# HGRN2 scores of distance 1 and 2 from channel products and a matrix of ones, in a streaming encoder step

## The chip, the cores and the metric

The kernel runs on one core of a Trainium2 chip. The metric is the time of one execution on the device, in microseconds (us). Three runs of the kernel before took 1739.62, 1742.65 and 1743.55 us; their median, 1742.65 us, is the time before.

## What is computed

The reference is one layer of a streaming encoder: an input projection of 2048 prompt frames and 8 x 16 sample frames, stick-breaking attention in 8 heads, an HGRN2 recurrence in 4 heads of 128 channels, an output projection and a LayerNorm. The change touches the HGRN2 part alone:

```
b = jnp.cumsum(gc, axis=2)                                  # g = log f
diff = b[:, :, :, None, :] - b[:, :, None, :, :]
decay = jnp.where(causal, jnp.exp(jnp.minimum(diff, 0.0)), 0.0)
scores = jnp.einsum('bhtd,bhsd,bhtsd->bhts', qc, kc, decay)
o = (jnp.einsum('bhts,bhsv->bhtv', scores, ic)
     + jnp.einsum('bhtd,bhdv->bhtv', qc * jnp.exp(b), S))
```

A score of the pair (s, t) is a sum over 128 channels of q[t] k[s] times the product of the forget gates f after s up to t.

## The kernel before, in words

The program has three stages: the input projection with the HGRN2 work woven into it (to about 1000 us), the stick-breaking attention, and the output projection. Only the first is touched.

**Projection.** The frames are taken in two halves. Each half has three tiles of tokens: 384, 384 and 384 in the first (the last 128 of these are the sample frames), 384, 384 and 256 in the second. The list `order` holds sections of 128 output columns (FH, QH, GH of a head, KA, QA, GA of attention) or of 256 (IH, VA). Each tile of a section takes 24 fp32r matmuls, since weight and input are split in a rounded part and a rest: 128x384 at L313 to L315, or 128x256 at L323 to L325 for IH and VA. After each 9, 9 and 6 of the first kind, or each 12 of the second kind, the loop calls `weave`. After the first tile of a section, `split_w` splits the weights of the next one: ScalarE copies (L109, `wh`), GpSimd takes the difference (L117, `wl`): two pairs of 128x512 for a section of 128 columns, four for one of 256. Sections KA and QA also split their output in this way (`e`).

**Chains.** When the GH section of a head is done, three generators `hgrn` are appended to `chains`, one per tile. `weave` takes the next step (up to the next `yield`) of the first chain, then puts that chain behind the second one. So two chains, here called A and B, go step by step in turn, and the third, C, begins when they end and goes alone, one step per `weave`. There are 4 heads x 2 halves = 8 pairs and 8 lone chains, 24 in all. All instructions are queued in the order in which Python issues them (`manual_schedule`), and each engine takes its own in that order.

**Levels.** A chunk of 128 tokens is worked level by level with distances m = 1, 2, 4, ..., 64. In each level, `scores` multiplies kS and q of a chunk in full fp32 (a 128x128 matmul, L430, two instructions each), then VectorE scales half of q and half of kS by the gate products of that level (L455, L456), keeps those scores that belong to the level by a mask (`copy_predicated`, L447) and forms the next gate products (L459). The diagonal is handled apart: the product dp = q kS (L423) is split in dh (ScalarE, fp32r) and dl = dp - dh (GpSimd, L466), and after the last level two matmuls with a matrix of ones sum dh and dl over the channels (L469, L470), masked into the scores at L471. The tile `ps` of these matmuls has two buffers for all chains together.

Of the kernel before, what the change touches and what calls it, by code (L numbers as in the profile page):

```python
# [9 lines left out]
F32 = mybir.dt.float32  # L10
F32R = mybir.dt.float32r
# [37 lines left out]
def constants():  # L49
    i = np.arange(P)  # L50
    s, t = i[:, None], i[None, :]
    x = s ^ t
    lev = np.stack([(s < t) & (x >= m) & (x < 2 * m) for m in LEVELS[:NL]] + [s == t], 1)
# [12 lines left out]
def stream_step_kernel(ctx: ExitStack, tc: tile.TileContext, x_prompt, x_sample, cache_k, cache_v, state_s,  # L66
# [19 lines left out]
    lev = cst.tile([P, NL + 1, P], U8, name="lev")  # L86
    hmask = cst.tile([P, H], F32, name="hmask")

    qT_d = scr.tile([4, 2, P, T], F32, name="qT_d")
# [44 lines left out]
    def bc(ap, n):  # L134
        return ap.unsqueeze(2).to_broadcast([ap.shape[0], ap.shape[1], n])
# [29 lines left out]
    def at(step, fn):  # L165
        todo.setdefault(max(step, -LZ - 9), []).append(fn)
# [31 lines left out]
    with ExitStack() as ph:  # L198
# [206 lines left out]
        def hgrn(half, h, hg, t0, nch):  # L405
# [13 lines left out]
            dp = hw.tile([P, TW], F32, name="dp", tag="kN")[:, :n]  # L419
            dh = hw.tile([P, TW], F32R, name="dh", tag="dh")[:, :n]  # L420
            dl = hw.tile([P, TW], F32R, name="dl", tag="dl")[:, :n]
            pool.memset(sc[:, :nch], 0.0)
            dve.tensor_tensor(dp, q, kS, ALU.mult)  # L423
            dve.tensor_tensor(q, q, f, ALU.mult)
            yield

            def scores(k):
                ps = psc.tile([P, 4, P], F32, name="ps", tag="ps")
# [1 line left out]
                    mm(ps[:, c], ch(kS, c), ch(q, c), start=True, stop=True)  # L430
                return ps[:, :k]

            tot = f
            tot16 = None
            for li, m in enumerate(LEVELS):
                k = nch if m < TS else npr
                if m < BLK:
                    ps = scores(k)
                else:
                    ps = psc.tile([P, 4, P], F32, name="ps", tag="ps")  # L440
                    for s0_ in range(0, P, 2 * m):
                        for c in range(k):
                            mm(ps[s0_:s0_ + m, c, :m], kS[:, c * P + s0_:c * P + s0_ + m],
                               q[:, c * P + s0_ + m:c * P + s0_ + 2 * m], start=True, stop=True)
                def keep_scores():
                    if m < BLK:
                        dve.copy_predicated(sc[:, :k], lev[:, li:li + 1].to_broadcast([P, k, P]), ps)  # L447
# [4 lines left out]
                q4 = q[:, :nn].rearrange("p (b two m) -> p b two m", two=2, m=m)  # L452
                k4 = kS[:, :nn].rearrange("p (b two m) -> p b two m", two=2, m=m)
                t3 = tot[:, :nn // m].rearrange("p (b two) -> p b two", two=2)
                dve.tensor_tensor(q4[:, :, 1], q4[:, :, 1], bc(t3[:, :, 0], m), ALU.mult)  # L455
                dve.tensor_tensor(k4[:, :, 0], k4[:, :, 0], bc(t3[:, :, 1], m), ALU.mult)  # L456
                keep_scores()
                nt = hw.tile([P, TW // 2 // m], F32, name=f"tot{m}", tag=f"tot{m}")[:, :nn // (2 * m)]
                dve.tensor_tensor(nt, t3[:, :, 0], t3[:, :, 1], ALU.mult)  # L459
                tot = nt  # L460
                if m == 8:
                    tot16 = nt
# [78 lines left out]


        def small():
            levf = xr.tile([P, NB, P], F32, name="levf", tag="x")[:, :NL + 1]
# [757 lines left out]
```

## Time and profile before

| | us |
|---|---|
| median of three runs | 1742.65 |
| lowest, highest | 1739.62, 1743.55 |
| the profiled execution | 1747.05 |
| its span, first to last instruction | 1745.2 |

The profiled execution is 4.40 us above the median, and 1.85 us of its time lie outside its span. Its page lists the busy time of the engines: PE is TensorE's matmuls, PEld its weight loads, DVE VectorE, ACT ScalarE, POOL GpSimd, SP the queue that issues the DMAs. Matmuls are pipelined, and the time of one is that from its start to its last result, so the rate is read from the distance of their starts. The mean granted TensorE clock of the execution is 0.989 of full speed.

### The profile page before, as it was taken

The page shows a single profiled execution, that of the slowest core. Times are in us where ns is not written, and L with a number is a line of the kernel's source. Part 1 is how long each engine was busy: PE and PEld are TensorE (multiplying, and loading weights), DVE is VectorE, ACT ScalarE, POOL GpSimd, SP SyncE. Part 2 cuts the span into 40 slices and gives each one's busy share as a digit, 9 for nine tenths or more (in the row PEclk, how much of TensorE's full clock was granted, in tenths as well). Part 3 has the DMA queues.
Part 4 walks back from the last instruction along what each step waited for, and adds up shares of the span by engine and source line. Part 5 has one row for each costly group of instructions (what it writes and reads, how often), then busy time and mean ns, then how long its engine had stood idle before and what let it go on. Part 6 is the DMA issues. An engine that isn't in the chain of part 4 may idle for free.

```text
span 1745.2 us, 33561 instructions
## 1 busy us (share of the span) xinstructions
PE 1672.4 (96%) x12901; PEld 1519.8 (87%) x12901; DVE 971.0 (56%) x1762; ACT 710.9 (41%) x1641; POOL 776.6 (44%) x870
## 2 busy tenths in 40 slices
PE   8999999999989999999999978999999999999998
PEld 8999999999989999999999966877887777778886
DVE  4264444255634263641647337787887686665554
ACT  3231221221323132221223246777877897775110
POOL 1242313232341142221323346777777776665664
PEclk9999999999999999999999989999999999999999
DMA  4233132122345133231212388899795754431443
GB/s 156 62 108 105 61 98 81 41 72 67 94 129 166 37 110 87 67 111 43 73 51 90 111 208 168 195 206 237 166 222 123 216 160 113 100 89 60 133 146 115
DMA packets 298790, 204.12 MB, mean 117 GB/s; under 512 B 113532, under 2 KB 275848, under 8 KB 298632
## 3 DMA queue, kind: packets, MB, share of 16 engines
q1 hardware_dynamic: 298632, 201.98, 43.5%
q8 instruction: 103, 1.69, 0.4%
q14 instruction: 55, 0.45, 0.1%
HBM read 146.36 MB, written 56.10 MB: 116 GB/s over the span
## 4 chain that ended last, share of the span: by engine, by line
PE 81%; DVE 5%; ACT 4%; DMA 4%; issue 2%; POOL 2%; SPq 1%; POOLq 0%; DVEq 0%; ACTq 0%
PE pj L313 10%; PE pj L315 10%; PE pj L314 10%; PE po L795 6%; PE z L742 5%; PE wt L777 5%; PE ps L430 4%; PE pj L323 4%; PE pj L325 4%; PE pj L324 4%; PE py L1132 3%; PE py L1134 3%; PE py L1133 3%; PE pk L877 2%; DVE kS L456 2%
## 5 line engine op out<-in xcount | busy, mean ns | idle before, releaser
L313 PE MATMUL pj<-xh,wh 128*128 128x384 f32 (+1 forms) x1152 | 395.7, 343 | 0.0
L764 POOL TENSOR_TENSOR s<-s,pr 128x512 f32<-128x512 f32 (+3 forms) x320 | 324.1, 1019 | 120.0 <-DVE pr L711 97.9
L315 PE MATMUL pj<-xh,wl 128*128 128x384 f32 (+1 forms) x1152 | 376.2, 327 | 0.0
L314 PE MATMUL pj<-xl,wh 128*128 128x384 f32 (+1 forms) x1152 | 375.7, 326 | 0.0
L117 POOL TENSOR_TENSOR wl<-wr,wh 128x512 fp32r<-128x512 f32 x126 | 164.2, 1327 | 387.9 <-ACT wh L109 387.9
L711 DVE TENSOR_TENSOR_SCAN pr<-keep,pr,one 128x513 f32<-128x513 f32 x192 | 238.6, 1270 | 46.7 <-ACT keep L750 35.0
L313 PEld LDWEIGHTS pj<-xh,wh 128*128 128x128 f32 x1152 | 217.4, 189 | 3.0 <-issue 1.0
L314 PEld LDWEIGHTS pj<-xl,wh 128*128 128x128 f32 x1152 | 217.5, 189 | 0.7 <-issue 0.7
L315 PEld LDWEIGHTS pj<-xh,wl 128*128 128x128 f32 x1152 | 216.7, 188 | 0.0
L742 PE MATMUL z<-kst,qr 128*128 128x512 f32 (+3 forms) x640 | 187.6, 404 | 17.9 <-ACT keep L750 6.3
L109 ACT COPY wh<-wt 128x512 f32<-128x512 f32 (+3 forms) x320 | 165.9, 550 | 78.4 <-PE wt L777 76.7
L747 ACT ACTIVATE s<-z 128x512 f32<-128x512 f32 (+3 forms) x320 | 184.6, 577 | 16.3 <-PE z L744 9.7
L777 PE MATMUL wt<-ident,s 128*128 128x128 f32 x1088 | 165.0, 279 | 2.1 <-POOL s L764 1.9
L323 PE MATMUL pj<-wh,xh 128*128 128x256 f32 x544 | 161.2, 296 | 0.0
L324 PE MATMUL pj<-wl,xh 128*128 128x256 f32 x544 | 153.0, 281 | 0.8 <-POOL wl L117 0.8
L777 PEld LDWEIGHTS wt<-ident,s 128*128 128x128 f32 x1088 | 123.2, 142 | 34.9 <-issue 16.4
L325 PE MATMUL pj<-wh,xl 128*128 128x256 f32 x544 | 152.8, 281 | 0.0
L117 POOL TENSOR_TENSOR e<-ev,e 128x384 fp32r<-128x384 f32 (+1 forms) x48 | 45.3, 943 | 221.1 <-ACT e L109 152.4
L795 PEld LDWEIGHTS po<-wh,vst 128*64 128x64 f32 x2176 | 119.1, 138 | 26.4 <-issue 16.2
L742 PEld LDWEIGHTS z<-kst,qr 128*128 128x128 f32 x640 | 106.0, 197 | 39.7 <-ACT keep L750 19.9
L795 PE MATMUL po<-wh,vst 128*64 128x128 f32 x2176 | 138.5, 279 | 0.0
L750 ACT ACTIVATE keep<-z 128x512 f32<-128x512 f32 (+2 forms) x230 | 134.6, 585 | 0.0
(164 smaller groups left out, 2907.0 us busy)
## 6 DMA issues: line engine op xcount, KB each, us to landing
wr<-in_w_in SPq DMA_DIRECT2D x64, 512.0 KB
qr<-qT_d SPq DMA_DIRECT2D x64, 256.0 KB
kr<-in_cache_k SPq DMA_DIRECT2D x16, 1024.0 KB
vr<-in_cache_v SPq DMA_DIRECT2D x32, 512.0 KB
kst<-kT_d SPq DMA_DIRECT2D x24, 512.0 KB
mt<-mx_d SPq DMA_DIRECT2D x136, 64.0 KB
x<-in_x_prompt SPq DMA_DIRECT2D x16, 512.0 KB
out<-xr SPq DMA_DIRECT2D x16, 512.0 KB
```

What stands on the lines that cost most here:

```text
L117: eng_lo.tensor_tensor(lo, src, f32(hi), ALU.subtract)
L313: mm(o, wh[:, k], xh[:, k, :n], start=k == 0, stop=False)
L314: mm(o, wh[:, k], xl[:, k, :n], start=False, stop=False)
L315: mm(o, wl[:, k], xh[:, k, :n], start=False, stop=k == KT - 1)
L323: mm(o, xh[:, k, ts], wh[:, k], start=k == 0, stop=False)
L324: mm(o, xh[:, k, ts], wl[:, k], start=False, stop=False)
L325: mm(o, xl[:, k, ts], wh[:, k], start=False, stop=k == KT - 1)
L711: dve.tensor_tensor_scan(pr[:, CW - wd:CW + 1][:, ::-1], kr, by, carry, ALU.mult, ALU.bypass)
L742: mm(z[:, :wd], q[:, a, r, q0:q0 + P], k[:, a, k0:k0 + wd], start=r == 0, stop=r == 1 and not top)
L764: pool.tensor_tensor(s[:, :wd], s[:, :wd], pr[:, CW - wd + 1:CW + 1], ALU.mult)
L777: nc.tensor.transpose(pt_[:, x:x + P], U[(u, a)][0][:, x:x + P], ident)
L795: mm(o[r], v[:, lo // P % 8 + x, r], th[a][:, x * P:(x + 1) * P], start=top and x == 0, stop=bot and x == n - 1, skip_group_check=True)
```

## The change

The scores of levels 1 and 2 are no longer taken from full matmuls. For level 1, the elementwise product of the odd tokens' q and the even tokens' kS (half the columns) is split in dh and dl and summed over channels by two matmuls with the matrix of ones. For level 2, there are four pairs per block of four tokens, so the product has as many columns as the tile. A column sum stands in all 128 rows of the result, and masks pick the row of s for each t: one `copy_predicated` for level 1, two per chunk for level 2. The diagonal's sums move from the last step to the first ones, and the same three tiles dp, dh, dl now serve all three sums in turn (`split` is the copy on ScalarE and the difference on GpSimd of the kernel before). Levels from 4 up are as before. The number of steps of a chain stays the same.

```diff
-            dve.tensor_tensor(dp, q, kS, ALU.mult)
+            def parts(w, out, a, b):
+                dve.tensor_tensor(out, a, b, ALU.mult)
+                split(act, pool, dh[:, :w], dl[:, :w], dp[:, :w])
+
+            def sums(w):
+                ps = psc.tile([P, 4, P], F32, name="ps", tag="ps").rearrange("p c t -> p (c t)")[:, :w]
+                mm(ps, ones, dh[:, :w], start=True, stop=False)
+                mm(ps, ones, dl[:, :w], start=False, stop=True)
+                return ps
+
+            def pick(i, out, cols, data):
+                dve.copy_predicated(out, lev[:, i, cols].unsqueeze(1).to_broadcast([P, nch, 64]), data)
...
+            parts(n, dp[:, :n], q, kS)
             dve.tensor_tensor(q, q, f, ALU.mult)
             yield
+            ps = sums(n)
+            dve.copy_predicated(sc[:, :nch], lev[:, 0:1].to_broadcast([P, nch, P]), ps.rearrange("p (c t) -> p c t", t=P))
+            parts(n // 2, dp[:, :n // 2], pair(q)[:, :, 1], pair(kS)[:, :, 0])
+            scale(n, 1, pair(f))
+            tot = total(1, n, pair(f))
+            yield
+            ps = sums(n // 2)
+            pick(1, sc[:, :nch, 1::2], slice(1, P, 2), ps.rearrange("p (c t) -> p c t", t=64))
+            q4, k4 = (z.rearrange("p (b two m) -> p b two m", two=2, m=2) for z in (q, kS))
+            sh = [P, n // 4, 2, 2]
+            parts(n, dp[:, :n].rearrange("p (b t s) -> p b t s", t=2, s=2),
+                  q4[:, :, 1].unsqueeze(3).to_broadcast(sh), k4[:, :, 0].unsqueeze(2).to_broadcast(sh))
+            scale(n, 2, pair(tot))
+            tot = total(2, n, pair(tot))
+            yield
+            ps = sums(n).rearrange("p (b t s) -> p b t s", t=2, s=2)
+            s4 = sc[:, :nch].rearrange("p c (b two t) -> p (c b) two t", two=2, t=2)
+            for a in range(2):
+                m4 = lev[:, 2 + a].rearrange("p (b two t) -> p b two t", two=2, t=2)[:, :, 1]
+                for c in range(nch):
+                    bs = slice(c * 32, (c + 1) * 32)
+                    dve.copy_predicated(s4[:, bs, 1], m4, ps[:, bs, :, a])
...
             for li, m in enumerate(LEVELS):
+                if m < 4:
+                    continue
...
-                if m == 2:
-                    copy(act, dh, dp)
-                if m == 4:
-                    pool.tensor_tensor(dl, dp, f32(dh), ALU.subtract)
                 yield
-            ps = psc.tile([P, 4, P], F32, name="ps", tag="ps")[:, :nch]
-            mm(ps, ones, dh, start=True, stop=False)
-            mm(ps, ones, dl, start=False, stop=True)
-            dve.copy_predicated(sc[:, :nch], lev[:, NL:NL + 1].to_broadcast([P, nch, P]), ps)
```

`scale` and `total` hold the two scalings and the gate products that stood in the loop over levels. The masks are reordered and one is added.

The change alters the order on the queues. GpSimd's queue, in the section KA behind the first head's GH, where chains A and B begin (`sc` is the score tile, `wl` the rest of the next section's weights, `e` that of the KA output; two `dl` in a row are A's and B's). Before:

```order
L422 MEMSET sc 128x384 x2
L117 TENSOR_TENSOR e_916<-ev,e_916 128x384
L117 TENSOR_TENSOR wl<-wr,wh 128x512 x2
L117 TENSOR_TENSOR e_987<-ev,e_987 128x384
L466 TENSOR_TENSOR dl<-dp,dh 128x384 x2
L117 TENSOR_TENSOR e_1057<-ev,e_1057 128x256
```

Now:

```order
L423 MEMSET sc 128x384
L118 TENSOR_TENSOR dl<-dp,dh 128x384
L423 MEMSET sc 128x384
L118 TENSOR_TENSOR dl<-dp,dh 128x384
L118 TENSOR_TENSOR dl<-dp,dh 128x192
L118 TENSOR_TENSOR e_922<-ev,e_922 128x384
L118 TENSOR_TENSOR dl<-dp,dh 128x192
L118 TENSOR_TENSOR wl<-wr,wh 128x512 x2
L118 TENSOR_TENSOR dl<-dp,dh 128x384 x2
```

A chain has three differences in place of one; the last two of the pair (level 2) stand behind the weights' `wl`, and the matmuls that read them belong to the next step of their chain.

VectorE's queue, in the first two level steps of the first lone chain (section VA). Before:

```order
L455 TENSOR_TENSOR hq<-hq,hf 128x192
L456 TENSOR_TENSOR kS<-kS,hf 128x192
L447 COPY_PREDICATED sc<-lev,ps 128x384
L459 TENSOR_TENSOR tot_1516<-hf 128x192
L455 TENSOR_TENSOR hq<-hq,tot_1516 128x96x2
```

Now:

```order
L454 COPY_PREDICATED sc<-lev,ps 128x384
L426 TENSOR_TENSOR dp<-hq,kS 128x192
L441 TENSOR_TENSOR hq<-hq,hf 128x192
L442 TENSOR_TENSOR kS<-kS,hf 128x192
L446 TENSOR_TENSOR tot_1538<-hf 128x192
L436 COPY_PREDICATED sc<-lev,ps 128x192
L426 TENSOR_TENSOR dp<-hq,kS 128x384
L441 TENSOR_TENSOR hq<-hq,tot_1538 128x96x2
L442 TENSOR_TENSOR kS<-kS,tot_1538 128x96x2
L446 TENSOR_TENSOR tot_1563<-tot_1538 128x96
L474 COPY_PREDICATED sc<-lev,ps 128x32x2 x6
```

The product dp now stands in each of the first three steps, behind the mask that reads the sums of the product before it, and the scalings stand behind dp.

## Rows read from the trace of the kernel before

**Rows 1.** The page: busy time, share of the span and instructions of each engine.
```profile
PE 1672.4 (96%) x12901; PEld 1519.8 (87%) x12901; DVE 971.0 (56%) x1762; ACT 710.9 (41%) x1641; POOL 776.6 (44%) x870
```

**Rows 2.** Windows: stretch, its length, busy us (instructions) PE PEld DVE ACT POOL, clock, DMA.
```profile
100.00:150.00 50.00, 49.42 (x400) 47.64 (x399) 26.30 (x67) 13.41 (x38) 17.11 (x25) 1.00 0.44 125
```

**Rows 3.** The page: shares of the chain that ended last, by line.
```profile
PE pj L313 10%; PE pj L315 10%; PE pj L314 10%; PE po L795 6%; PE z L742 5%; PE wt L777 5%; PE ps L430 4%; PE pj L323 4%; PE pj L325 4%; PE pj L324 4%; PE py L1132 3%; PE py L1134 3%; PE py L1133 3%; PE pk L877 2%; DVE kS L456 2%
```

**Rows 4.** Timeline of PE: start us, us, engine, line, operation, count.
```profile
94.36 0.83 PE L430 MATMUL ps<-hq,kS 128*128 128x128 f32 x6
...
95.20 0.33 PE L314 MATMUL pj<-xl,wh 128*128 128x384 f32 x1
95.38 0.34 PE L315 MATMUL pj<-xh,wl 128*128 128x384 f32 x1
...
300.00 0.28 PE L323 MATMUL pj<-wh,xh 128*128 128x256 f32 x1
300.12 0.28 PE L324 MATMUL pj<-wl,xh 128*128 128x256 f32 x1
```

**Rows 5.** Groups by form: busy us, mean ns | idle before, releasers.
```profile
L430 PE MATMUL ps<-hq,kS 128*128 128x128 f32 x672 | 95.4, 276 | 12.0 <-DVE kS L456 8.4 <-DVE sc L447 2.6 <-DVE tot L459 1.1
...
L447 DVE COPY_PREDICATED sc<-lev,ps 128x384 f32<-128x384 uint8 x96 | 56.3, 586 | 0.0
...
L447 DVE COPY_PREDICATED sc<-lev,ps 128x256 f32<-128x256 uint8 x24 | 10.6, 443 | 0.0
...
L455 DVE TENSOR_TENSOR hq<-hq,hf 128x192 f32<-128x192 f32 x20 | 7.2, 358 | 7.2 <-PE ps L430 7.2
...
L423 DVE TENSOR_TENSOR dp<-hq,kS 128x384 f32<-128x384 f32 x20 | 11.2, 558 | 0.7
...
L109 ACT CAST dh<-dp 128x384 fp32r<-128x384 f32 x20 | 9.4, 511 | 0.0
...
L109 ACT CAST e<-ev 128x256 fp32r<-128x256 f32 x16 | 6.5, 406 | 0.5
...
L466 POOL TENSOR_TENSOR dl<-dp,dh 128x384 fp32r<-128x384 f32 x20 | 21.1, 1072 | 6.8 <-ACT dh L109 6.8
...
L466 POOL TENSOR_TENSOR dl<-dp,dh 128x256 fp32r<-128x256 f32 x4 | 3.0, 762 | 6.6 <-ACT dh L109 6.6
...
L117 POOL TENSOR_TENSOR wl<-wr,wh 128x512 fp32r<-128x512 f32 x126 | 164.2, 1327 | 387.9 <-ACT wh L109 387.9
...
L117 POOL TENSOR_TENSOR e<-ev,e 128x384 fp32r<-128x384 f32 x32 | 33.3, 1041 | 159.3 <-ACT e L109 129.6 <-issue 29.8
```

**Rows 6.** Timelines of DVE, PE and POOL, the first lone chain.
```profile
138.53 0.56 DVE L423 TENSOR_TENSOR dp<-hq,kS 128x384 f32<-128x384 f32 x1
...
140.31 0.83 PE L430 MATMUL ps<-hq,kS 128*128 128x128 f32 x6
...
142.38 0.83 PE L430 MATMUL ps<-hq,kS 128*128 128x128 f32 x6
...
143.49 1.02 POOL L466 TENSOR_TENSOR dl<-dp,dh 128x384 fp32r<-128x384 f32 x1 [6.81 <-ACT dh L109]
...
143.52 1.20 DVE L456 TENSOR_TENSOR kS<-kS,tot 128x192 f32<-128x192 f32 x1
```

**Rows 7.** Timelines of DVE, PE and POOL, the first pair of chains.
```profile
84.66 0.56 DVE L423 TENSOR_TENSOR dp<-hq,kS 128x384 f32<-128x384 f32 x1
...
86.14 0.83 PE L430 MATMUL ps<-hq,kS 128*128 128x128 f32 x6
...
90.19 2.76 POOL L117 TENSOR_TENSOR wl<-wr,wh 128x512 fp32r<-128x512 f32 x2
```

**Rows 8.** PE's waits from 80 to 1000 us: us in total, times, longest.
```profile
PE ps L430 <- DVE kS L456: 8.4, 9, 1.4
...
PE ps L430 <- DVE sc L447: 2.6, 2, 1.3
```

**Rows 9.** Windows: one stretch of 5 us, columns as in rows 2.
```profile
520.00:525.00 5.00, 2.79 (x4) 1.25 (x5) 0.68 (x3) 0.00 (x0) 2.15 (x2) 0.68 0.63 210
```

More of the change, by code (lines that the diff above doesn't have):

```diff
@@ L52, in constants @@
     x = s ^ t
-    lev = np.stack([(s < t) & (x >= m) & (x < 2 * m) for m in LEVELS[:NL]] + [s == t], 1)
+    at = lambda m: (s < t) & (x >= m) & (x < 2 * m)
+    lev = np.stack([s == t, at(1), at(2) & (s % 2 == 0), at(2) & (s % 2 == 1)] + [at(m) for m in LEVELS[2:NL]], 1)
     f = lambda a: np.ascontiguousarray(a, dtype=np.float32)
@@ L85, in stream_step_kernel @@
     pool.memset(f32(ones), 1.0)
-    lev = cst.tile([P, NL + 1, P], U8, name="lev")
+    lev = cst.tile([P, NL + 2, P], U8, name="lev")
     hmask = cst.tile([P, H], F32, name="hmask")
@@ L418, in hgrn @@
             sc = hw.tile([P, 3, P], F32, name="sc", tag="sc")
-            dp = hw.tile([P, TW], F32, name="dp", tag="kN")[:, :n]
-            dh = hw.tile([P, TW], F32R, name="dh", tag="dh")[:, :n]
-            dl = hw.tile([P, TW], F32R, name="dl", tag="dl")[:, :n]
+            dp = hw.tile([P, TW], F32, name="dp", tag="kN")
+            dh = hw.tile([P, TW], F32R, name="dh", tag="dh")
+            dl = hw.tile([P, TW], F32R, name="dl", tag="dl")
             pool.memset(sc[:, :nch], 0.0)
-            dve.tensor_tensor(dp, q, kS, ALU.mult)
+            def parts(w, out, a, b):
+                dve.tensor_tensor(out, a, b, ALU.mult)
+                split(act, pool, dh[:, :w], dl[:, :w], dp[:, :w])
@@ new lines, in sums, with scale @@
+            def sums(w):
[5 more added lines that the diff above has]
+                dve.copy_predicated(out, lev[:, i, cols].unsqueeze(1).to_broadcast([P, nch, 64]), data)
+            def scale(a, m, t3):
+                a4 = lambda z: z[:, :a].rearrange("p (b two m) -> p b two m", two=2, m=m)
+                q4, k4 = a4(q), a4(kS)
+                dve.tensor_tensor(q4[:, :, 1], q4[:, :, 1], bc(t3[:, :, 0], m), ALU.mult)
+                dve.tensor_tensor(k4[:, :, 0], k4[:, :, 0], bc(t3[:, :, 1], m), ALU.mult)
@@ L424, in hgrn, with total @@
+            def total(m, a, t3):
+                nt = hw.tile([P, TW // 2 // m], F32, name=f"tot{m}", tag=f"tot{m}")[:, :a // (2 * m)]
+                dve.tensor_tensor(nt, t3[:, :, 0], t3[:, :, 1], ALU.mult)
+                return nt
+            pair = lambda z: z.rearrange("p (b two) -> p b two", two=2)
+            parts(n, dp[:, :n], q, kS)
             dve.tensor_tensor(q, q, f, ALU.mult)
             yield
+            ps = sums(n)
+            dve.copy_predicated(sc[:, :nch], lev[:, 0:1].to_broadcast([P, nch, P]), ps.rearrange("p (c t) -> p c t", t=P))
@@ L431, in scores @@
                 return ps[:, :k]
-            tot = f
             tot16 = None
             for li, m in enumerate(LEVELS):
+                if m < 4:
+                    continue
                 k = nch if m < TS else npr
@@ L446, in keep_scores @@
                     if m < BLK:
-                        dve.copy_predicated(sc[:, :k], lev[:, li:li + 1].to_broadcast([P, k, P]), ps)
+                        dve.copy_predicated(sc[:, :k], lev[:, li + 2:li + 3].to_broadcast([P, k, P]), ps)
                         return
@@ L451, in hgrn @@
                 nn = k * P
[L452 to L456, printed above, removed]
+                t3 = pair(tot[:, :nn // m])
+                scale(nn, m, t3)
                 keep_scores()
-                nt = hw.tile([P, TW // 2 // m], F32, name=f"tot{m}", tag=f"tot{m}")[:, :nn // (2 * m)]
-                dve.tensor_tensor(nt, t3[:, :, 0], t3[:, :, 1], ALU.mult)
-                tot = nt
+                tot = total(m, nn, t3)
                 if m == 8:
-                    tot16 = nt
-                if m == 2:
-                    copy(act, dh, dp)
-                if m == 4:
-                    pool.tensor_tensor(dl, dp, f32(dh), ALU.subtract)
+                    tot16 = tot
                 yield
-            ps = psc.tile([P, 4, P], F32, name="ps", tag="ps")[:, :nch]
-            mm(ps, ones, dh, start=True, stop=False)
-            mm(ps, ones, dl, start=False, stop=True)
-            dve.copy_predicated(sc[:, :nch], lev[:, NL:NL + 1].to_broadcast([P, nch, P]), ps)
             pk = pt.tile([P, 4, P], F32, name="pk", tag="pt")
@@ L543, in small @@
         def small():
-            levf = xr.tile([P, NB, P], F32, name="levf", tag="x")[:, :NL + 1]
+            levf = xr.tile([P, NB, P], F32, name="levf", tag="x")[:, :NL + 2]
             dma.dma_start(levf, levels_d)
```

## The prediction

> **What bounds the kernel now.** I read the page's busy times first: PE is busy in 96% of the span [rows 1]. Next the windows of the stage that the change touches: PE 49.4 of 50 us, VectorE 26, ScalarE 13, GpSimd 17, clock 1.00, DMA share 0.44 [rows 2]. So this stage lasts as long as TensorE's queue, and the other engines have idle time in sum. The chain that ended last says the same: projection and score matmuls lead it, and the scores of L430 alone hold 4% [rows 3]. Then the waits: over some 900 us, PE waited 8.4 us for the scaled kS and 2.6 us for a buffer of the scores [rows 8]. PE takes its instructions in order, so each such wait delays all that follows. Hence the two questions: how much PE work goes, and how often PE must now wait for what the other engines make.
>
> **PE work removed.** Two of the five levels with full matmuls go. The stage has 68 chunks (half 1: 9 for each of 4 heads; half 2: 8), so 2 x 68 matmuls of two instructions, 272 of the 672 recorded [rows 5]. The row's 276 ns is a latency; the price is the distance of starts. Six instructions and one projection matmul take from 94.36 to 95.20, 0.84 us; the next projection matmul comes 0.18 later [rows 4]. So six cost 0.67, one 0.11, and 272 x 0.11 = **30 us** go.
>
> **PE work added.** A 128x384 fp32r matmul costs 0.17 to 0.18, a 128x256 one 0.12 [rows 4]. For the 192 columns of level 1 I take 0.10, a bit under the 256 row; its bounds are 0.09 (the columns' share) and 0.12, 0.8 us over all. A chain of 384 tokens adds 2 x 0.18 + 2 x 0.10 = 0.56, one of 256 adds 2 x 0.12 + 2 x 0.08 = 0.40; 20 and 4 chains: **13 us**. The diagonal's two matmuls only move. Net on PE: **-17 to -18 us**.
>
> **The waits added.** Before, dh and dl of the diagonal were made some five steps before PE read them. Now three times per chain a product goes VectorE, ScalarE, GpSimd, and PE needs it in the chain's next step. Prices [rows 5]: product of 384 columns 0.56, of 192 0.36; ScalarE copy 0.51, and by the line through 384 and 256 columns 0.35 for 192; difference 1.07, and likewise 0.61; mask 0.59 for 384, 0.44 for 256, so 0.37 for 192 and about 0.23 for the 64 of each small mask. I add nearly 0.1 for each hand-over.
>
> *Lone chain, 384 tokens* [rows 6]. PE took the steps at 140.31 and 142.38: 2.07 apart, 0.67 of it scores and 1.4 projection. Step 1: the product ends at 139.09; copy and difference end near 141.2; PE's second sum (dl) is due at 140.49: waits 0.7. Step 2: from the start of that sum it takes 0.34 (result), 0.5 (mask), 0.36, 0.35, 0.61 and the hand-overs, 2.4 to 2.5; PE's own work until it needs it is 0.17 + 1.4 + 0.1: waits 0.7. Step 3: 0.25, 0.37, 0.56, 0.51, 1.07 and hand-overs, 2.9, against 1.65: waits 1.2. Step 4 scales kS behind six small masks, ready about when PE comes. Sum 2.6 us, against 0.8 us of PE work saved. With 256 tokens the same steps give 1.3, against 0.5.
>
> GpSimd's queue adds to some of these (its new order shows what stands between two differences of a lone chain). In two of the first half's four lone chains an `e` difference (1.04) does: 3.6 each. In the second half one has an `e` (2.2), and one has four weight differences of 1.33 between the first and the second: about 5. The eight: 2 x 2.6 + 2 x 3.6 + 2 x 1.3 + 2.2 + 5 = **22 us**.
>
> *Pair* [rows 7]. Two steps in turn leave about twice the time. Still, A's first product ends at 85.22, so dl is ready near 86.95, and PE is due at 86.14 + 0.18: 0.6. B's first product falls under A's difference: a VectorE product of two SBUF inputs stretches there, as 1.20 for kS against 0.36 shows [rows 5, 6]; B's sums wait 0.75, its level 1 sums 0.45. The large one comes at level 2: A's and B's differences stand behind two weight differences (2.76 [rows 7]). With B's level 1 difference ending near 93.1, the weights end near 95.8 and A's difference near 96.9, while PE is due near 94.4 (where it was at 94.36 [rows 4]): 2.4. Sum 4.2 us for six of the pairs, against 1.6 saved. In the two pairs whose next section is 256 columns wide, four weight differences stand there (5.3): the same walk gives 0.6 + 0.3 + 0.2 + 5.2 = 6.3. All pairs: 6 x 4.2 + 2 x 6.3 = **38 us**.
>
> *Waits that go.* PE's present waits at L430 are 12 us in all [rows 5]; levels 1 and 2 hold a part that I can't separate. Bounds 0 and 12; I take **6**.
>
> **The rest.** VectorE's own time grows by some 1.3 us per chain (a product more of 0.56 and one of 0.36, masks 0.37 + 6 x 0.23 for 2 x 0.59, the copy being ScalarE's); it has half its time free [rows 2], so its sum costs nothing, and the part on the path is in the walks. The same holds for ScalarE (+0.86 per chain) and GpSimd (+1.7). No DMA is added. `split_w` is late by the differences ahead of it, about 2 us in a section of 12 or more, which hides it. The later stages shift as a whole.
>
> **A rule that speaks against the change.** The product above stretches while GpSimd works. The Trainium skill (SBUF — State Buffer, "SBUF: two separate sides") says that a VectorE instruction with two SBUF inputs and a GpSimd one that reads SBUF exclude each other for a whole instruction. By that rule alone each added difference may hold VectorE for its length, an estimate of 20 x 1.68 + 4 x 1.27 = 39 us; by the rows it costs VectorE only where a product was waiting, which is what the walks take. The trace agrees with the rule in kind.
>
> **Clock.** A 5 us wait may cost more than itself: where PE was busy 2.79 of 5 us, the granted clock was 0.68 [rows 9], so part of that stretch ran at 1.2 GHz instead of 2.4. I add nothing for the three waits of about 5 us, and up to 4 us to the range. The Trainium skill (TensorE: Matmul & The Clock Gate, Part 1) says that idling lowers the clock and activity raises it again; by it those waits would each bring such a stretch.
>
> **Sum.** -30 + 13 + 22 + 38 - 6 = **+37**, say +36 us. The profiled execution would go from 1747.05 to 1783; it lies 4.4 above the median of the runs, 1742.65, from which I forecast **1779 us**.
>
> **Rivals.**
> 1. *The turns hide it, and the kernel gets faster.* If each product came back within the work that PE has between two steps of a chain (2.07 us alone, some 4 us in a pair), only the PE sum would be left: 1742.65 - 17.6 = 1725. For it: PE's waits now are small [rows 8], and three engines are half idle [rows 2]. Against it: step 3 of a lone chain needs 2.9 us by plain durations with no queue in the way. 12%.
> 2. *Only the lone chains and the first hand-overs wait.* If GpSimd's weight differences finish before A's level 2 product arrives, the waits of 2.4 (six) and 5.2 (two) fall away: 25 less, +11, 1754. It is decided by whether B's level 1 difference, ahead of the weights in the queue, comes early. 20%.
> 3. *VectorE becomes the bound in the steps of level 2 and 4.* Six small masks of 0.23 and two scalings stretched by about 1.1 each under the weight differences would delay kS for both chains of a pair: 8 x 2 x 1.1 = 17 more, 1796. For it: 1.20 against 0.36 [rows 5, 6]. Against: the mean stretch is smaller, and PE will already be waiting then. 15%.
> 4. *The change doesn't remove what it says.* The instruction order has 200 full score matmuls where it had 336, so this is excluded.
>
> **How the numbers follow.** The main case holds 49%, with a range of its own from 1765 to 1792 (half the waits that go, 0.1 us per hand-over in 72, the clock). Rivals 1 to 3 hold 12, 20 and 15%, and no change 4%, if the waits happen to eat exactly the saving. The range of 8 in 10 takes in rivals 2 and 3 and leaves out rival 1 and no change: **1748 to 1802**. About 0.2% is what a measurement of this kernel can tell from no change; faster 0.12, same 0.04, slower 0.84.
>
> **What would show it.** Right: L430's successor with 400 recorded instructions; new PE waits at the sums, for dl on GpSimd above all, 72 places at most and some 50 to 60 us in all; the largest behind `wl` in the section after GH; in the lone chains waits of 0.7 to 1.2 three times; the first stage ending 30 to 40 us later with the rest unchanged. Wrong: the sums' waits under 20 us in total, or a first stage that ends earlier; or waits for VectorE (kS, masks) larger than those for GpSimd.

## The result, and the profile after

The changed kernel takes **1794.29 us**, the median of five runs (1792.20 to 1796.94), against 1742.87 us for the kernel before in the same rounds: 1.0299 times as long, with a 95% interval from 1.0284 to 1.0314, or 51.4 us more. (The two new runs of the kernel before moved its median from 1742.65.) The forecast was 1779, with a range from 1748 to 1802. The profiled execution of the changed kernel took 1793.25 us, 46.2 more than the profiled one of before.

The page of the changed kernel: the busy row, and the chain that ended last, by engine and by line.

```profile
PE 1684.9 (94%) x12725; PEld 1512.8 (84%) x12725; DVE 1000.2 (56%) x1922; ACT 731.2 (41%) x1689; POOL 815.2 (46%) x918
...
PE 76%; DVE 9%; ACT 5%; DMA 4%; issue 3%; POOL 3%; SPq 1%; POOLq 0%; ACTq 0%; DVEq 0%
PE pj L314 9%; PE pj L316 8%; PE pj L315 8%; PE po L832 6%; PE z L779 5%; PE wt L814 5%; PE py L1169 4%; PE py L1171 3%; PE py L1170 3%; PE pj L324 3%; PE pj L326 3%; PE pj L325 3%; PE ps L479 3%; DVE dp L426 2%; PE pk L914 2%
```

PE has 176 instructions fewer than in [rows 1] (272 for scores gone, 96 for sums added), and yet its share fell from 96 to 94%. The scores' share of the chain fell from 4% [rows 3] to 3% (L479 is L430's successor), and VectorE's product L426 stands in it now.

Where the time went is read from the last projection matmul, which ends the first stage. The timeline of PE, before:

```profile
1007.46 0.28 PE L315 MATMUL pj<-xh,wl 128*128 128x256 f32 x1
```

In the changed kernel (last row below) it starts at 1055.03, 47.6 us later. So the whole loss lies in the first stage, and the later ones only shift. Timelines of DVE, PE and POOL of the changed kernel, merged: the first pair, the first lone chain, the end of the stage.

```profile
91.23 2.94 POOL L118 TENSOR_TENSOR wl<-wr,wh 128x512 fp32r<-128x512 f32 x2
91.79 1.26 DVE L426 TENSOR_TENSOR dp<-hq,kS 128x384 f32<-128x384 f32 x1
...
93.08 1.31 DVE L441 TENSOR_TENSOR hq<-hq,tot 128x192 f32<-128x192 f32 x1
...
93.70 0.45 PE L431 MATMUL ps<-dh,ones 128*128 128x384 f32 x1 [0.61 <-ACT dh L110]
94.14 1.10 POOL L118 TENSOR_TENSOR dl<-dp,dh 128x384 fp32r<-128x384 f32 x1
...
94.31 1.15 DVE L442 TENSOR_TENSOR kS<-kS,tot 128x192 f32<-128x192 f32 x1
...
95.30 0.44 PE L432 MATMUL ps<-dl,ones 128*128 128x384 f32 x1 [1.15 <-POOL dl L118]
...
142.98 0.34 PE L431 MATMUL ps<-dh,ones 128*128 128x384 f32 x1
143.77 0.44 PE L432 MATMUL ps<-dl,ones 128*128 128x384 f32 x1 [0.46 <-POOL dl L118]
...
146.25 0.36 PE L432 MATMUL ps<-dl,ones 128*128 128x192 f32 x1 [0.32 <-POOL dl L118]
...
148.27 0.44 PE L431 MATMUL ps<-dh,ones 128*128 128x384 f32 x1 [0.26 <-ACT dh L110]
...
149.36 0.45 PE L432 MATMUL ps<-dl,ones 128*128 128x384 f32 x1 [0.65 <-POOL dl L118]
...
1055.03 0.28 PE L316 MATMUL pj<-xh,wl 128*128 128x256 f32 x1
```

A bracket gives the engine's idle time before the row and what ended it; for PE it counts only from the modelled end of the matmul ahead. The sum over dl at 143.77 was due 0.17 after the one over dh at 142.98, so it is 0.62 late and shows 0.46. Read in this way the three steps of the lone chain lose 0.6, 0.6 and 1.4 us. In the pair the large one comes where the walk put it: A's level 2 difference (94.14) stands behind the two weight differences (91.23), and PE's two matmuls come late: the one over dh by 0.8, because the product at 91.79 was stretched to 1.26, and the one over dl by 1.4.

PE's waits from 80 to 1050 us, with their number and the longest, against [rows 8]:

```profile
PE ps L432 <- POOL dl L118: 32.9, 43, 3.8
PE ps L431 <- ACT dh L110: 8.9, 16, 1.0
PE ps L479 <- DVE kS L442: 3.0, 5, 1.5
...
PE ps L479 <- DVE sc L436: 2.4, 6, 0.4
```

At the sums PE has 41.8 us of recorded idle time in 59 waits, 43 of them (32.9 us) for GpSimd's dl; the old waits for kS and for the buffer shrank from 11.0 to 5.4 us. Two groups by form:

```profile
L479 PE MATMUL ps<-hq,kS 128*128 128x128 f32 x400 | 61.5, 291 | 6.6 <-DVE kS L442 3.0 <-DVE sc L436 2.4 <-DVE sc L497 0.7
...
L426 DVE TENSOR_TENSOR dp<-hq,kS 128x384 f32<-128x384 f32 x40 | 35.2, 879 | 0.7
```

400 instructions are left of 672 [rows 5], and a product of 384 columns takes 0.88 us on average, where the one of before took 0.56 [rows 5]: 20 of the 40 take 0.56 to 0.58, and the other 20, stretched, 0.91 to 1.28.

Windows of the changed kernel, columns as in [rows 2]: the ten microseconds from the start of the first pair, then stretches of 5 us further on in the first pair and in the second.

```profile
82.53:92.53 10.00, 9.00 (x50) 8.12 (x49) 9.79 (x19) 3.68 (x8) 5.94 (x7) 1.00 0.10 39
...
90.00:95.00 5.00, 3.41 (x19) 2.65 (x17) 4.93 (x8) 1.91 (x4) 4.33 (x4) 1.00 0.21 80
95.00:100.00 5.00, 4.26 (x16) 4.01 (x17) 4.62 (x17) 1.78 (x4) 2.37 (x3) 0.67 0.49 144
210.00:215.00 5.00, 4.08 (x24) 3.53 (x22) 4.93 (x10) 2.95 (x6) 3.06 (x4) 1.00 0.10 39
215.00:220.00 5.00, 1.15 (x4) 0.89 (x5) 4.97 (x7) 0.25 (x1) 4.24 (x4) 0.62 0.47 124
220.00:225.00 5.00, 5.00 (x26) 5.00 (x26) 3.90 (x21) 0.65 (x2) 1.01 (x1) 0.70 0.38 129
```

Two things stand here that the prediction's sum did not have. First, the clock: after PE was busy 1.15 of 5 us, the next 5 us, fully busy, were granted 0.70, so part of them ran at 1.2 GHz instead of 2.4. In the kernel before one such stretch lay in the first stage [rows 9]; now eleven windows of 5 us are below 0.97. Weighted with PE's busy time in them (the sum of one minus the clock, times the busy time) they cost about 13 us, against 0.9 before. Second, VectorE: it was busy 9.79 of 10 us, and it is the same in all eight pairs.

### The profile page after: what moved, and what is told of

It is laid out like the page before. It is cut to its first block, busy times and chain, and to the rows that moved or that the text cites. A ratio compares the mean times of both kernels' runs of the same rounds, so it can differ in the third digit from the quotient of the medians.

```text
span 1791.5 us, 33420 instructions
## 1 busy us (share of the span) xinstructions
PE 1684.9 (94%) x12725; PEld 1512.8 (84%) x12725; DVE 1000.2 (56%) x1922; ACT 731.2 (41%) x1689; POOL 815.2 (46%) x918
## 4 chain that ended last, share of the span: by engine, by line
PE 76%; DVE 9%; ACT 5%; DMA 4%; issue 3%; POOL 3%; SPq 1%; POOLq 0%; ACTq 0%; DVEq 0%
PE pj L314 9%; PE pj L316 8%; PE pj L315 8%; PE po L832 6%; PE z L779 5%; PE wt L814 5%; PE py L1169 4%; PE py L1171 3%; PE py L1170 3%; PE pj L324 3%; PE pj L326 3%; PE pj L325 3%; PE ps L479 3%; DVE dp L426 2%; PE pk L914 2%
## 5 line engine op out<-in xcount | busy, mean ns | idle before, releaser
L118 POOL TENSOR_TENSOR dl<-dp,dh 128x384 fp32r<-128x384 f32 (+3 forms) x72 | 61.9, 859 | 140.1 <-ACT dh L110 134.8
```

## The experiments

The expectations call their theories by letters. A is the prediction's: PE waits for the way from VectorE over ScalarE and GpSimd back to PE. B is that VectorE's own added work binds (rival 3). E came up behind the first misses: GpSimd's differences cost twice, as a hand-over and by what they do to VectorE's queue. C is that the change removes less PE work than was worked out, D that something other than longer chains eats the saving. For runs with one execution the time of that one is given. The stages that no edit touches, from the last projection matmul to the end, took 731 to 738 us in these executions, so where a difference is small the start of that matmul is compared as well. Line numbers shift with each edit; the tiles tell which instruction a row is.

**Three empty steps.** One `yield` more in front of each of the three sums, so that PE has one more slice of projection before it needs them; no work changes. The first of the three:

```diff
             yield
+            yield
             ps = sums(n)
```

> Theory A (round trip): PE waits because a product has to come back from VectorE, ScalarE and GpSimd within one step of its chain. Three empty steps per chain, one in front of each pair of summing matmuls, change no instruction, only give each product two turns instead of one. Then the recorded waits at the summing matmuls fall from about 42 us to under 12, the half-clock stretches of the first stage go except one or two, and the time falls to about 1740 us (1728 to 1755), near the kernel before. Theory B (VectorE is the bound, by a product, masks and stretched scalings more): the work is the same, so the time stays above 1785. Theory C (the PE work saved is smaller than 17 us): the waits go, but the time stays above 1760.

Measured: 1741.11 us (eight runs, 1737.56 to 1743.17), 0.9976 of before (0.9963 to 0.9990). PE's waits in the stage, and the window at the start of the first pair:

```profile
PE pq L562 <- DVE on L558: 10.2, 5, 3.4
PE xT L305 <- DMA x<-in_x_prompt: 6.2, 3, 3.0
...
PE ps L432 <- POOL dl L118: 1.6, 4, 0.6
```

```profile
82.63:92.63 10.00, 10.00 (x60) 9.97 (x59) 8.49 (x14) 3.33 (x7) 6.85 (x7) 1.00 0.13 46
```

With the same work on every engine the whole loss is gone: 53 us for three empty steps. So the loss is time of arrival, not work, and the sums' 41.8 us became 1.6. Theory A's number came. Of the 17 us that PE saves in matmuls little is kept. Longer chains leave steps for the end of a half, and PE waits longer there for `on` (10.2 against 2.6 us) and the next x; that this eats the saving is not shown. But the step gives time to every engine ahead of PE, to VectorE also (8.49 of 10 us, with PE at 10.00), so it does not tell which of them was late.

**The differences on VectorE.** `split(act, dve, ...)` for the three products, in place of GpSimd.

```diff
-                split(act, pool, dh[:, :w], dl[:, :w], dp[:, :w])
+                split(act, dve, dh[:, :w], dl[:, :w], dp[:, :w])
```

> The three differences dl of a chain on VectorE instead of GpSimd, nothing else. Theory A: the differences no longer stand behind the next section's weight differences, and one of 384 columns takes some 0.56 instead of 1.07 us, so the large waits (2 to 5 us, in the pairs) go; VectorE waits some 0.6 us for each copy instead. About 20 to 25 us less than the changed kernel: 1770 (1760 to 1782). Theory B: VectorE gets 24 x 1.5 = 36 us more work and stands still at each copy, so the time grows to 1805 or more.

Measured: 1812.6 us, the slowest of all. PE's waits:

```profile
PE ps L431 <- ACT dh L110: 32.2, 33, 2.6
PE ps L479 <- DVE kS L442: 7.3, 8, 1.5
PE ps L479 <- DVE sc L436: 7.2, 8, 1.6
```

Theory A was missed by 43 us, and Theory B's number (1805 or more) came. VectorE takes its instructions in order and now stands at each difference until ScalarE's copy is there; the next product, and with it the next copy, comes late: VectorE waits 41.5 us for dh at its 72 differences. PE's waits for dl fell to 4.0 us, and those for dh have taken their place.

**One small mask of six.** Of the masks of level 2 only the first is left, so most of the scores of level 2 are not picked.

```diff
-                for c in range(nch):
+                for c in range(1):
                     bs = slice(c * 32, (c + 1) * 32)
-                    dve.copy_predicated(s4[:, bs, 1], m4, ps[:, bs, :, a])
+                    if a == 0:
+                        dve.copy_predicated(s4[:, bs, 1], m4, ps[:, bs, :, a])
```

> Leaves out five of the six small masks of level 2 (four of five with 256 tokens differ: three of four), so most scores of distance level 2 stay zero; about 20 us of VectorE work less. Theory A: PE waits for GpSimd, and the masks come after the sums have arrived; only the wait for kS behind them shrinks: 0 to 8 us less, 1786 to 1794. Theory B: 20 us or more less, 1775 or below.

Measured: 1788.07 us, in Theory A's range; the last projection matmul starts 0.9 us earlier than in the changed kernel, and the waits for dl stayed at 32.8 us in 43 places. The small masks are not what PE waits for.

**The price of the scores.** The kernel before without the score matmuls and masks of levels 1 and 2, whose scores are left out.

```diff
-                if m < BLK:
+                if m < 4:
+                    pass
+                elif m < BLK:
                     ps = scores(k)
...
-                keep_scores()
+                if m > 2:
+                    keep_scores()
```

> The kernel before without the score matmuls and masks of levels 1 and 2 (these scores stay zero), nothing in their place. It measures the PE work that the change removes. Prediction's price: 272 instructions at 0.11 = 30 us less, 1713 (1708 to 1718). Theory C: 20 us less or fewer, above 1722.

Measured: 1718.26 us. The last projection matmul starts at 981.08, 26.4 us earlier than before, with PE's waits for kS and the buffer at 13.9 us (13.5 and 0.4), 2.9 more than the 11.0 of [rows 8]. So the scores' own price is about 29 us, where the prediction had 30.

**The rest left out.** No dl at all: each product is rounded, and dh is summed twice, so the three sums lack the rest and count the rounded part double.

```diff
-                split(act, pool, dh[:, :w], dl[:, :w], dp[:, :w])
+                copy(act, dh[:, :w], dp[:, :w])
...
-                mm(ps, ones, dl[:, :w], start=False, stop=True)
+                mm(ps, ones, dh[:, :w], start=False, stop=True)
```

> Leaves out the differences: the second summing matmul reads the rounded dh once more, so the three sums are wrong by a factor of two; PE, VectorE and ScalarE work stay, GpSimd's 72 differences go. Theory A: a round trip is shorter by a difference and a hand-over (0.7 to 1.2) and free of GpSimd's queue; the waits at dl go, some 10 us of waits at dh stay: 1745 (1738 to 1756). Theory B: 1780 or above.

Measured: 1762.23 us, 32 under the changed kernel, 19 over the kernel before, between the numbers of the two theories. PE's waits:

```profile
PE ps L430 <- ACT dh L110: 17.2, 16, 2.7
...
PE ps L478 <- DVE sc L435: 6.5, 2, 3.2
PE ps L478 <- DVE kS L441: 4.6, 8, 1.5
```

And two rows of the merged timelines of its first pair:

```profile
90.33 1.25 DVE L425 TENSOR_TENSOR dp<-hq,kS 128x384 f32<-128x384 f32 x1
...
91.96 0.51 ACT L110 CAST dh<-dp 128x384 fp32r<-128x384 f32 x1 [3.17 <-DVE dp L425]
```

GpSimd's part is gone, and a good third of the loss is still there. Here ScalarE had stood idle for 3.17 us until VectorE's product came (stretched, beside `wl`), and the sum behind it starts at 92.53.

**The weights' differences later.** `split_w` behind the second tile of a section (`if ti == 1`) instead of the first, which takes `wl` out of the pairs' level 2.

```diff
-                if ti == (i == 0):
+                if ti == 1:
```

> The split of the next section's weights is issued behind the second tile of a section instead of the first, so the level 2 differences of a pair stand ahead of the weight differences in GpSimd's queue. Theory A: the pairs' large waits shrink by the length of the weight differences (2.65 or 5.3): 20 to 30 us less with the clock, 1768 (1760 to 1780), less what the projection may wait for late weights. If the round trip alone made those waits: 1788 or above.

Measured: 1783.47 us, 11 less than the changed kernel (6 of it in the first stage) where 26 was expected. The longest wait for dl fell from 3.8 to 1.3 us and the sum from 32.9 to 21.4, but there are still 43 of them, waits for masks and kS of VectorE grew from 6 to 15 us, and one wait for the second half's frames from 1.5 to 5.9. PE's recorded idle time from 80 us to the end of the stage is the same (55 against 56 us). The 5 us windows at a lower clock, weighted as above, cost 6 us in place of 13, and that is the stage's whole gain. The pair's large wait was rightly seen; what is freed there, other waits take up, those for VectorE above all.

**One empty step.** The extra `yield` in front of level 2's sums alone.

```diff
             yield
+            yield
             ps = sums(n).rearrange("p (b t s) -> p b t s", t=2, s=2)
```

> One empty step, in front of the sums of level 2 alone. Theory A with the prediction's terms: the waits at level 2 go (2.4 in six pairs, about 5 in two, 0.7 to 1.4 in the lone chains, some 32 us) and most half-clock stretches with them (up to 12 us), the smaller ones at the diagonal and level 1 stay: 1755 (1748 to 1768). If the waits at the diagonal and level 1 were the main part: above 1775.

Measured: 1779.95 us, 14 less (8 of it in the first stage), the alternative's number, with 27.3 us of waits for dl left in 34 places. Sorted by the level of the sum, those at level 2 fell from 18.3 to 5.1 us, as the step was meant to do, but those at the diagonal and level 1 grew from 14.5 to 22.2. So the alternative is not shown by its number: level 2 was the larger part, and most of what left it came back at the other two sums.

**Late sums.** The products are made as in the changed kernel, but the sums are read late, without a longer chain: the diagonal's one step later, level 1's behind level 16 (its dh and dl lie in a tile of tag `mo`), level 2's behind level 64.

```diff
-            ps = sums(n // 2)
-            pick(1, sc[:, :nch, 1::2], slice(1, P, 2), ps.rearrange("p (c t) -> p c t", t=64))
+            take0()
...
+                if m == 16:
+                    take1()
+                if m == 64:
+                    take2()
                 yield
```

> The sums are read late instead of by way of empty steps: the diagonal's one step later, level 1's after level 16 (from tiles of its own, in the space of a later tile), level 2's after level 64. No instruction is added. Theory A: no sum waits for its product any more, without the longer chains of the empty steps; PE keeps nearly all of its saving, so 1730 (1724 to 1738), faster than both kernels. Rival D (the empty steps' run kept only 3 of 17 us because something else, not the longer chains, eats the saving, such as VectorE's masks and scalings): 1739 to 1745 again.

Measured: 1792.04 us (five runs, 1791.0 to 1792.65), 1.0279 of before (1.0263 to 1.0295). This is the run that upset Theory A, and it is far above Rival D's number too. PE's waits, and the merged timelines of the first pair:

```profile
PE ps L488 <- DVE kS L444: 51.0, 19, 4.8
PE ps L433 <- DVE sc L509: 5.3, 6, 1.2
```

```profile
89.69 2.92 POOL L118 TENSOR_TENSOR wl<-wr,wh 128x512 fp32r<-128x512 f32 x2
...
90.34 1.14 DVE L428 TENSOR_TENSOR dp<-hq,kS 128x384 f32<-128x384 f32 x1
91.52 1.30 DVE L443 TENSOR_TENSOR hq<-hq,tot 128x192 f32<-128x192 f32 x1
...
92.74 1.14 DVE L444 TENSOR_TENSOR kS<-kS,tot 128x192 f32<-128x192 f32 x1
...
94.03 1.01 PE L488 MATMUL ps<-hq,kS 128*128 128x128 f32 x6 [4.24 <-DVE kS L444]
```

Not one wait for dl is left, and the time is nearly the same: PE now waits for VectorE's kS. While GpSimd works (89.69 on), a product of 384 columns takes 1.14 and two scalings of 192 columns take 1.30 and 1.14, against 0.56 and 0.36 [rows 5]. Behind the first limit lay a second one of nearly the same price, and the waits of the changed kernel had hidden it. That the two times agree so well is partly chance: the 5 us windows at a lower clock cost 20 us here against 13, so the waits themselves are some 10 us less.

**Late sums without the differences.** The late sums with the rest left out as above: both matmuls of a sum read dh. Against the late sums:

```diff
-                split(act, pool, dhs[j][:, :w], dls[j][:, :w], dp[:, :w])
+                copy(act, dhs[j][:, :w], dp[:, :w])
```

> The late sums without the differences (both summing matmuls read dh, the sums are wrong by a factor of two): GpSimd's 72 differences go, VectorE's work stays the same. Theory E: only the weight and output differences still stretch VectorE, and no product waits for a difference to free dp: 1748 (1738 to 1760). If VectorE's own added work makes the wait: 1780 or more.

Measured: 1749.24 us, as Theory E had it: 43 us less than the late sums with their differences (38.8 in the first stage). PE's first wait row reads as follows:

```profile
PE ps L487 <- DVE kS L443: 26.5, 22, 3.4
```

GpSimd's differences are read by nobody for several steps in the run above, so a wait of PE for dl has no part in these 43 us. They act on VectorE: by longer instructions, and by holding the tile dp. Up to the last projection matmul VectorE is busy 513.7 us with the differences and 482.8 without them, 31 us more for the same instructions, and it waited 10.0 us for a difference before it could write dp again. So the stretch is the larger of the two on VectorE; how much of each reached PE the runs don't separate. Of the 38.8 us, the windows at a lower clock are 16 (20 against 4), which come behind PE's waits.

Taken together, the four runs cross two edits. With the differences, late reading is worth 2 us (1794 to 1792); without them, 13 (1762 to 1749). Leaving the differences out is worth 32 us when the sums are read on time and 43 when late. So the differences are the larger part of the loss, and where no sum waits for them any more, they still cost the time by way of VectorE.

**Late sums, weights later** (the edits of the two runs together), and **three empty steps at a higher rate** (the three empty steps with the constant `HRATE` of the weaving at 1.15, to have the chains end earlier).

```diff
-HRATE = 1.0
+HRATE = 1.15
```

> The late sums, and the weights' split issued behind the second tile instead of the first. In the run with the late sums no sum waited for its product, but the level 4 scores waited 51 us for kS, whose scaling stood in VectorE's queue behind masks and products stretched while GpSimd worked. Theory E (the wait for GpSimd has two ways to PE: by the sums, and by VectorE's stretched products): without the weight differences in that place the waits for kS halve, 1760 (1750 to 1772). If VectorE's own added work makes the wait: 1780 or more.

> The three empty steps per chain, and the chains take 1.15 steps per turn of the projection instead of 1, so that the longer chains of the last two heads of a half end before the half does. In the run with the empty steps some 10 us went where left-over steps ran without projection work between them (500 to 600 us: PE busy 84 of 100). Theory A: that goes, the waits at the sums stay small: 1733 (1728 to 1740), faster than the kernel before. If the two steps that now sometimes follow in one turn bring the waits back: 1742 or more.

Measured: 1785.94 us, and 1764.12 us (five runs, 1760.84 to 1765.83; 1.0116 of before, 1.0097 to 1.0135). Both missed, and both times the alternative's number came. With the first, 32.9 us of waits for kS stayed, where the changed order was to halve the 51.0. With the second, steps come closer together and the sums' waits are back (dl 8.3 us in 15 places), with 13.5 us at kS and gate products; the waits for `on`, which the higher rate was to remove, stayed at 10.0 us. Of the 53 us that the empty steps had won, 23 are lost again when the steps follow faster.

**Sums in full precision.** The sums of levels 1 and 2 straight from the product, one fp32 matmul of two instructions with the ones, so that nothing goes over ScalarE and GpSimd; the diagonal as in the kernel before.

```diff
+            d1 = hw.tile([P, TW], F32, name="d1", tag="mo")
...
-                split(act, pool, dh[:, :w], dl[:, :w], dp[:, :w])
...
-                mm(ps, ones, dh[:, :w], start=True, stop=False)
-                mm(ps, ones, dl[:, :w], start=False, stop=True)
+                mm(ps, f32(ones), d1[:, :w], start=True, stop=True)
```

> The sums of levels 1 and 2 are taken in full fp32 straight from the product (one fp32 matmul with the ones, of 2 instructions, no copy on ScalarE and no difference on GpSimd; the product lies in the space of tile mo). The diagonal is as in the kernel before: split late, summed at the end. TensorE pays an estimated 24 x 0.96 = 23 us (a pass of full precision at 384 and 192 columns put at 0.64 and 0.32 us, from the matmuls of the profile) for the 25 to 30 that go; the product comes back to TensorE in one hand-over; GpSimd and ScalarE keep the work of before. Theory A (the way over ScalarE and GpSimd, and what it stretches on VectorE, is the cause): waits at the sums under 10 us in all, time 1740 (1734 to 1750). Rival (VectorE's own added work, the product and the six small masks, is the bound): 1765 or above.

Measured: 1781.32 us (five runs, 1779.56 to 1785.19), 1.0221 of before (1.0205 to 1.0236): the rival's number. PE's waits in the stage, the first pair's window, and merged timelines of the pair:

```profile
PE ps L431 <- DVE d L427: 13.9, 10, 3.3
PE ps L477 <- DVE kS L441: 11.9, 9, 1.9
PE ps L431 <- DVE sc L472: 7.5, 4, 2.1
PE ps L477 <- DVE sc L435: 7.4, 8, 2.8
```

```profile
81.64:91.64 10.00, 8.94 (x51) 8.27 (x49) 9.76 (x21) 4.25 (x9) 4.10 (x4) 1.00 0.18 50
```

```profile
92.45 2.40 POOL L507 TENSOR_TENSOR dl<-dp,dh 128x384 fp32r<-128x384 f32 x2
92.93 1.05 DVE L440 TENSOR_TENSOR hq<-hq,tot 128x192 f32<-128x192 f32 x1
93.90 1.17 DVE L441 TENSOR_TENSOR kS<-kS,tot 128x192 f32<-128x192 f32 x1
...
95.16 0.99 DVE L472 COPY_PREDICATED sc<-lev,ps 128x64 f32<-128x64 uint8 x6
...
96.29 0.88 PE L431 MATMUL ps<-d,ones 128*128 128x384 f32 x2 [1.62 <-DVE sc L472]
```

All four rows of waits name VectorE: for the product, the scaling, and masks that free the buffer `ps`. With no way over ScalarE and GpSimd at levels 1 and 2 the stage's last projection matmul is still at 1043.94, 36.5 us late. The sum at 96.29 waits for the six masks of the other chain, and these stand behind two scalings that the diagonal's differences (92.45) have stretched to three times their length. The full precision costs PE an estimated 23 of the 29 us, so this is no cheap variant; but the 41 us of waits don't come from PE's work. Nor are they VectorE's added work alone, as the rival has it: GpSimd's differences for the diagonal still stretch its instructions.

The windows of all pairs show how full VectorE is. Ten microseconds from the instruction that makes A's kS in a pair, means over the pairs (eight; six with empty steps, where two more do not start together), busy us:

| kernel | PE | VectorE |
|---|---|---|
| before | 9.99 | 9.26 |
| changed | 9.15 | 9.79 |
| rest left out | 8.86 | 9.76 |
| late sums | 8.22 | 9.76 |
| late sums without differences | 8.46 | 9.76 |
| full precision | 8.69 | 9.77 |
| three empty steps | 10.00 | 8.56 |

They don't show the loss: the late sums without their differences have PE less busy there than the changed kernel has, and took 45 us less. That shows in the next five microseconds (10 to 15 from the same instruction, means over eight pairs): PE is busy 4.64 of 5 before, 2.18 in the changed kernel, 2.50 with late sums, and 4.80 with late sums without differences; VectorE 4.68, 4.94, 4.96 and 4.71. The row of the kernel before for its first pair, ten microseconds, is this one:

```profile
84.27:94.27 10.00, 10.00 (x69) 9.97 (x68) 9.19 (x22) 2.86 (x6) 3.79 (x3) 1.00 0.12 44
```

## Why the prediction was right, and where it was not

**Direction and size.** Slower was right, and the time lies inside the range, 2.3 us above the main case's own. Between the profiled executions the sum was +37, and +46.2 came. The other 5 or so of the 15 us to the median are no mechanism: the profiled execution of before lay 4.4 above its median, that of the changed kernel 1.0 below.

**PE work removed and added.** Right: 30 us, and the run without these scores shows 29. The added sums take what the walk took, 0.17 between the starts at 384 columns.

**The walks.** Right where they can be read. Lone chain: predicted 0.7, 0.7 and 1.2, found 0.6, 0.6 and 1.4. First pair: predicted 4.2, found about 4.4 (0.7, 0.5, 0.3 and 2.2 at the four places, and 0.7 for the buffer `ps` at 96.17, which was not in the walk). Read in the same way at all sums of the stage, an estimate from the distances of starts, the lone chains lose 21 us and the pairs 36, where the walks had 22 and 38, and the waits that go came to 5.6, where 6 was taken. The terms 22, 38 and -6 make +54; with 47.6 in the stage, -16 of PE's matmuls and +12 of the clock, about 52 is left for all waits.

**Clock: the term that was mis-sized.** "I add nothing for the three waits of about 5 us, and up to 4 us to the range." It cost about 12. The step counted only the few long waits. The stretches below full clock come at seven places, and four of these are pairs whose longest waits were to be 2.4 us, where several short waits follow one another (95 to 100 us above: 0.67, behind waits of 0.6 and 1.2 us). The three places that the step had in mind cost 5.6 us, the four others 7.3. The Trainium skill (TensorE: Matmul & The Clock Gate, Part 1) says that an idle TensorE falls back to 1.2 GHz. The trace agrees in kind: PE was busy 3.41 of the 5 us ahead of that stretch, and 1.15 of the 5 us in which the clock fell in the second pair.

**VectorE: the argument that did not hold.** The prediction says of VectorE that "it has half its time free [rows 2], so its sum costs nothing". The window of [rows 2], 100 to 150 us, leaves out the start of the first pair (84.27): it holds that pair's later levels and the first 12 us of a lone chain. In a pair's first ten microseconds VectorE was already busy 9.26 of 10 us before the change; 1.3 us of work more per chain, and longer instructions beside GpSimd's differences, had no room there. So rival 3's mechanism is real in part: the scalings under `wl` are stretched as it said (1.31 and 1.15 at 93.08 and 94.31, 0.95 and 0.79 longer, where it put 1.1), but the small masks alone cost nothing. Its number, 1796, lies nearer than the forecast, and that is luck: its sign, waits for kS, came to 3.0 us in the changed kernel. It did not show in the time because PE was already waiting for GpSimd: the two limits have nearly the same price. The sign given for being wrong, waits for VectorE larger than those for GpSimd, did not come (5.4 against 32.9 us); the wait rows of one profile name what came last, not what would come next.

**GpSimd.** Waits for dl above all, 43 of the 59 recorded at the sums, the largest behind `wl`: as forecast. But by the prediction's own reasoning the time should fall when the sums are read later, and it did not: the waits for dl went, and the late sums still took 1792. What the differences cost VectorE is the missing part: without them the time is 32 us less when sums are read on time, 43 when late. For the rule on the shared side of SBUF (the Trainium skill, SBUF — State Buffer, "SBUF: two separate sides") the prediction had an estimate of 39 us, for the 48 added differences, if it bound everywhere, and took the rows' smaller effect. The two runs leave out all 72 differences, 61.9 us of GpSimd's time, and VectorE's instructions became 31 us shorter in sum with late sums, 18 with sums on time (490.5 to 472.0): the traces agree with the rule in kind, at half of that time or less.

**Rivals 1 and 2** are out: PE waits 41.8 us at the sums, and A's level 2 difference does stand behind `wl`. Where the empty steps hid the sums' waits the time was that of before, not 1725, and the weights' differences out of the way gave 1783, not 1754.

**What stays open.** How the 43 us divide between stretched instructions and the late release of dp, as far as PE feels them; what makes the late sums without differences still 23 us slower than the 1726 that PE's matmuls alone would give; and why one empty step, the later weights and the full precision each gave less than was worked out: in each, other waits took up what was freed, but none isolates VectorE's part. No version clearly beat the kernel before: three empty steps gained 0.24%, barely over what can be told from no change.

## What to carry to other kernels

Read an engine's room in the stretch where the added work falls, here ten microseconds of a pair, not over a window that mixes it with idle ones: 53% and 93% were the same engine. Before trusting that a named wait is the bound, ask what is late next; one run that takes the wait away without changing the work (empty steps) and one that only moves its reader (late sums) tell the two apart. Taking matmuls from the busiest engine pays only if the engines that feed it have room in those same microseconds.

## What the runs showed of the hardware

- A mask's time does not follow its columns alone: the pick of level 1, 192 columns with every second one written (L436), took 0.57 to 0.60 us, as much as the plain one of 384 (0.59 [rows 5]), where 0.37 was estimated; six masks of 64 columns (L474) took 1.0 us together, 0.17 each, where 0.23 was.
- The clock fell behind several short waits as well as behind a long one: eleven windows of 5 us lie below 0.97 in the stage against one before, and the longest recorded waits ahead of the stretch at 95 to 100 us are 0.6 and 1.2 us.
- A VectorE product of two SBUF inputs went from 0.56 to between 0.91 and 1.28 us, and a scaling of 192 columns from 0.36 to between 1.05 and 1.31, while a GpSimd difference ran beside it; half of the changed kernel's 40 products of 384 columns were stretched.
